# Up-projection of a channel mixer: products that go on accumulating in banks that were read, and sums moved from GpSimd to VectorE

## Chip, cores and metric

One core of one Trainium2 chip runs the kernel. The metric is the device time of one execution in microseconds (us); the profile is one execution with the hardware profiler on. Engines by their names in the profile: PE is TensorE, DVE is VectorE, ACT is ScalarE, POOL is GpSimd, SP the queue that issues most DMAs.

## What is computed

The reference is a trunk of two layers over 1024 tokens of 1024 channels, each layer a mixer and then a channel mixer, all in float32. The change is in the channel mixer, which runs once in each layer:

```
def conv_glu_ffn(x, w_up, conv_w, conv_b, w_down):
    h = causal_dwconv(x @ w_up, conv_w) + conv_b        # w_up 1024 x 5632, width-3 convolution over tokens
    gate, up = jnp.split(h, 2, axis=-1)                 # 2816 columns each
    return (jax.nn.silu(gate) * up) @ w_down            # w_down 2816 x 1024
```

## The kernel before

Each float32 product is made of three passes on TensorE: operands are split into a high part (a copy rounded to the engine's format, on ACT) and a low part (source minus high part, on DVE), and `mm3` multiplies high by high, high by low and low by high.

The up-projection (`ffn`) goes through 22 tiles, c = 0 to 21. A tile is 128 gate columns and 128 value columns. Taken as 2 x 2 blocks, it costs seven block products in place of eight (Winograd's form of Strassen's scheme), numbered 1 to 7. Each block product is four steps of `mm3`, so 12 matmuls of 128 x 128 by 128 x 512 into one PSUM bank of 512 columns; a tile has 84 of them. The operands of the tokens (B11, B21, B22, T1 to T4) are ready in SBUF. Of the weights, three products take a loaded block (A11, A12, A22) and four take a sum of blocks, S1 to S4, which `block` makes with `tensor_tensor` on GpSimd (line 249), 128 x 512 each. `prep` then splits the operand (ACT line 257, DVE line 258), five products ahead of its use (`FLA`).

In `product`, products 2 and 3 go to the two halves of a tile of two banks, `w["A"]`, that becomes the gate; the others go to single banks, of which the pool has four. The blocks of the result are sums of several products, and DVE makes these sums: seven adds of 128 x 512 with one operand in PSUM in each tile (lines 282 to 289, 294, 298), behind one copy on ACT (line 280). Then `conv` makes the convolution, once for the gate from PSUM and once for the value from SBUF: one activation on ACT (line 262) and two `scalar_tensor_tensor` of 128 x 1024 on DVE (lines 263 and 264). ACT applies SiLU to the gate (line 296), GpSimd multiplies gate and value (line 300, 128 x 1024) and issues the store (line 301).

Tiles 0 and 1 go side by side in the order `FIRST`, while the operands T1 to T4 of the last half of the tokens are still being made (line 148 and line 214, the latter on GpSimd for T3 and T4). From tile 2 on, tiles go one after the other, products in the order 1, 6, 5, 2, 7, 3, 4. Every engine runs its own instructions strictly in the order that the scheduler of the framework wrote at build time; waits between engines are semaphores, and two engines never work on the same PSUM bank at once. The down-projection (`dn`) follows with PE work of its own.

Of the kernel before, what the change touches and what calls it, by code (L numbers as in the profile page):

```python
# [16 lines left out]
P = 128  # L17
# [46 lines left out]
class Kern:  # L64
# [73 lines left out]
    def mm3(self, ps, ah, al, bh, bl, first, last):  # L138
        nc = self.nc
        nc.tensor.matmul(ps, ah, bh, start=first, stop=False)  # L140
        nc.tensor.matmul(ps, ah, bl, start=False, stop=False)  # L141
        nc.tensor.matmul(ps, al, bh, start=False, stop=last)  # L142

    def split_half(self, src, s="x"):
        """hi and lo of one [128, 512] operand, side by side."""
        t = self.U(s, F32R)
        self.nc.scalar.copy(t[:, :512], src)  # L147
        self.nc.vector.tensor_sub(t[:, 512:], src, t[:, :512].bitcast(F32))  # L148
        return t
# [34 lines left out]
    def mixer_operands(self, zs, half, gname, bname, xo):  # L184
        """the blocks B11, B21, B22 and sums T1 to T4 that the up-projection takes, in high and low parts"""
        nc = self.nc
        lo, hi = slice(0, 512), slice(512, 1024)
        raw = [self.U("xr") for _ in range(4)]
        ts = [self.U("xt") for _ in range(4)] if half else None

        def put(name, src):
            xo.setdefault(name, []).append(self.split_half(src, "x"))

        for j in range(4):
            for k in range(2):
                kt = j + 4 * k
                ps = self.B("tp")
                for i in range(4):
                    nc.tensor.transpose(ps[:, i * P:i * P + P], zs[i][:, kt * P:kt * P + P], self.ident)
                dst = raw[j][:, (lo, hi)[k]]  # L200
                nc.scalar.activation(dst, ps, AF.Identity, bias=self.pc_(bname, kt), scale=self.pc_(gname, kt))  # L201
                if not half:
                    put(("B11", "B21")[k], dst)
        if not half:
            xo["raw"] = raw
            return
        old = xo["raw"]
        for name, d, x, y in (("B22", None, None, None), ("T1", lo, (raw, lo), (old, lo)), ("T2", hi, (raw, hi), (ts, lo)),
                              ("T3", lo, (raw, hi), (raw, lo)), ("T4", hi, (ts, hi), (old, hi))):
            for j in range(4):  # L210
                if d is None:
                    put(name, raw[j][:, hi])
                    continue
                (nc.gpsimd if name in TP else nc.vector).tensor_tensor(ts[j][:, d], x[0][j][:, x[1]], y[0][j][:, y[1]], op=ALU.subtract)
                put(name, ts[j][:, d])

# [1 line left out]
    def ffn(self, l, xo, resid, tail, nxt=None):  # L218
        """generator, one step for each block product of the up-projection. That takes a gate tile and a value tile of
        128 columns together: as 2 x 2 blocks (columns by halves of the channels, times halves of the channels by  # L220
        halves of the tokens) they come from seven block products, by Winograd's form of Strassen's scheme."""
# [11 lines left out]
        def block(c, name):  # L233
            """a block of the weights, or a sum of such"""
# [7 lines left out]
            if name not in w:  # L242
                x, y, op = sums[name]
                x, y = block(c, x), block(c, y)
                half = ("S12", "S34")[name in ("S3", "S4")]
                if half not in w:
                    w[half] = self.U("ws")
                w[name] = w[half][:, lo if name in ("S1", "S3") else hi]
                nc.gpsimd.tensor_tensor(w[name], x, y, op=op)
# [17 lines left out]
        def product(c, i):  # L267
            w = W[c]
            xn = prods[i][1]
# [3 lines left out]
            t = w.pop(i)  # L273
            for j in range(4):
                k, x = j * P, xo[xn][j]
                self.mm3(ps, t[:, k:k + P], t[:, 512 + k:512 + k + P], x[:, lo], x[:, hi], j == 0, j == 3)
            add = nc.vector.tensor_add
# [7 lines left out]
            if i == 7:  # L285
# [4 lines left out]
                w["gate"] = True  # L290
            if i == 5:
                w["p5"] = ps
            if i in (3, 7) and "gate" in w and not any(k in w for k in (3, 7)):
                add(w["A"][:, hi], w["A"][:, hi], w["u"][:, hi])  # L294
                w["g"] = conv(w["A"], c)
                nc.scalar.activation(w["g"], w["g"], AF.Silu)
            if i == 4:
                nc.vector.tensor_sub(w["h"][:, lo], w["u"][:, lo], ps)
                v = conv(w["h"], NC + c)
                nc.gpsimd.tensor_tensor(v, w["g"], v, op=ALU.mult)  # L300
                nc.gpsimd.dma_start(GS[c], v)
                W[c].clear()

        seq = [(c, i) for i in FIRST for c in range(2)]
        seq += [(c, i) for c in range(2, NC) for i in (1, 6, 5, 2, 7, 3, 4)]
# [74 lines left out]
    def make_tail(self, gi, bi, row, mode):  # L380
        """gi, bi: parameter names; row: (g, b) DRAM rows. Returns (tail, result)."""
# [5 lines left out]
        def tail(t, r, dh):  # L387
            """goes on with half dh of a tile of tokens"""
# [50 lines left out]
    def out_proj(self, w, yhl, resid, tail, in_w=(0, 1, 7), eng=None):  # L439
        """generator: loads the weights, then goes on by tiles of 128 tokens"""  # L440
# [21 lines left out]
    def mixer0(self, then):  # L462
# [61 lines left out]
        # generators of filling work: each step is one half of a column tile of the input projection  # L524
# [51 lines left out]
        # attention, one tile of 128 queries of one head after the other  # L576
# [27 lines left out]
        def turn(hd, i, p):  # L604
            """the weights of one tile, keys first"""
# [54 lines left out]
        # operands of the output projection: the last head's come two tiles at a time  # L660
# [31 lines left out]
        # queries and keys of the first head follow the input as it arrives  # L692
# [68 lines left out]
    def rwkv(self, xf, then):  # L761
# [29 lines left out]
        def variant(i, kt, x=None, h=None, eng=None):  # L791
            """x plus its mixed difference to the token before: of all tokens, or of one half of them"""
# [8 lines left out]
        def ahead(items, make, n=2):  # L801
            """items with what make gives for them, n of these in the making before one is used"""
# [16 lines left out]
        def spread(xs, i, src=None):  # L819
            """generator: the operands of a projection"""  # L820
# [15 lines left out]
        def lora1(steps):  # L836
            """generator: the first products of several low-rank maps, over the channel tiles"""
# [18 lines left out]
        def loras():  # L856
            """generator: hidden parts of the gate, the decay and the learning rate; the small ones in several copies
            over the partitions, so that products of high and low parts go in one pass"""
# [21 lines left out]
        def project(xs, w, evac, by_half=False, ws=None, pair=True):  # L880
            """generator: one projection; stops between the halves of a tile and behind each tile, and says where. The
            first two tiles go side by side, so that they can follow the operands as these are made, and with pair
            the last two, so that they give the operands' room back one by one"""
# [58 lines left out]
        # receptance, with the loras between its tiles; its start fills the gap behind what comes before  # L942
# [33 lines left out]
        def gates():  # L976
            """generator: the gate, written out for later"""
# [28 lines left out]
        # second lora weights: high and low parts stacked against the doubled hidden rows  # L1006
# [156 lines left out]
        # Of the four pairs of heads in a unit, the first two (s = 0) keep the state, b and u in partitions 0 to 63  # L1163
        # and k and v in the others, the last two (s = 1) the other way round.
        def chunk_operands(q, g, s, a):
            """b and k of two pairs of heads, and a (or r) of each head with zeros beside it"""
# [14 lines left out]
        def prepare1(q, g, u):  # L1181
            """generator: chunk matrices of one unit between a and b, k, and the inverses of their 32x32 diagonal blocks"""
# [44 lines left out]
        def prepare3(q, g, u):  # L1227
            """generator: chunk matrices of one unit between r and b, k, and the transposes of b, k"""
# [18 lines left out]
        def prepare2(q, g, u):  # L1247
            """generator: the whole 64x64 inverses, and the operands of the recurrence"""
# [46 lines left out]
        def chunks(work, pump):  # L1295
            """one chunk of 64 tokens of each unit in work; the chains of two units run side by side"""
# [53 lines left out]
        def finish(q, g, O):  # L1350
            """generator: group norm over the 64 channels of each head, then bonus and gate"""
# [107 lines left out]
def build(tc, ins, out, stop=None):  # L1459
    with ExitStack() as ctx:  # L1460
# [18 lines left out]
        def mixed(i, l, w, resid, alpha, out_args, last_tail, nxt=None):  # L1479
            """the output projection of the mixer of layer l, with the start of its channel mixer in the gap behind"""  # L1480
# [131 lines left out]
```

## Time and profile before

| what | us |
|---|---|
| three runs | 2848.95, 2855.28, 2872.17 |
| median of the runs | 2855.28 |
| span of the profiled execution, first to last instruction | 2858.8 |
| up-projection, tiles 2 to 20, layer 0 | 607.7 to 994.7 of the span |
| up-projection, tiles 2 to 20, layer 1 | 2202.7 to 2590.3 of the span |

The span is the profiled execution's own time as far as the profile shows it; it lies 3.5 us above the median and within the runs. The two stretches of the up-projection are cut at the ACT copies of line 280, which stand right behind product 1 of a tile, so each holds 19 whole tile periods.

### The profile page before, as it was taken

How to read it: one execution, taken by the hardware profiler on the slowest of the kernel's cores; microseconds unless marked ns; L12 is line 12 of the kernel's file. 1: busy time of each engine (PE TensorE's matmuls, PEld its weight loads, DVE VectorE, ACT ScalarE, POOL GpSimd, SP SyncE). 2: the span in 40 equal slices, each digit the busy share in tenths (PEclk: the TensorE clock that was granted, in tenths of full speed). 3: DMA queues.
4: the chain of work that ended last, by engine and by line, in shares of the span. 5: the costliest groups of instructions: out<-in, count | busy, mean ns of one | idle time of the engine just before them, and what ended most of it. 6: DMA issues, size and time to landing. Idle time of an engine off the chain costs nothing. (4 is left out here: it accounts for less than half of the span.)

```text
span 2858.8 us, 38102 instructions
## 1 busy us (share of the span) xinstructions
PE 2639.9 (92%) x14736; PEld 2140.1 (75%) x14736; DVE 2065.9 (72%) x2796; ACT 1060.9 (37%) x1650; POOL 850.0 (30%) x558
## 2 busy tenths in 40 slices
PE   8999989979998999999998998688897999899998
PEld 6777777768777788777876777577776787778886
DVE  4645656699999964657778656777759999997463
ACT  3323343234343441526665223334224344334330
POOL 0000003564554303010045211345555455441000
PEclk9999979999999999999997998787998999999999
DMA  5111233122222173543256779777431222224751
GB/s 163 52 45 52 63 114 104 67 74 74 82 83 71 67 231 115 195 158 111 89 188 217 230 219 232 175 175 204 154 125 48 93 78 78 82 74 158 240 187 41
DMA packets 208678, 358.10 MB, mean 125 GB/s; under 512 B 88945, under 2 KB 118257, under 8 KB 208497
## 3 DMA queue, kind: packets, MB, share of 16 engines
q1 hardware_dynamic: 198704, 320.01, 36.1%
q0 software_dynamic: 9792, 35.66, 3.4%
q8 instruction: 116, 1.90, 0.3%
q14 instruction: 66, 0.53, 0.1%
HBM read 255.46 MB, written 95.94 MB: 123 GB/s over the span
## 5 line engine op out<-in xcount | busy, mean ns | idle before, releaser
L140 PE MATMUL up<-x,wu 128*128 128x512 f32 x1232 | 485.3, 397 | 47.4 <-DVE u L282 22.4
L142 PE MATMUL up<-x,wu 128*128 128x512 f32 x1232 | 479.0, 397 | 10.3 <-DVE wu L258 10.2
L141 PE MATMUL up<-x,wu 128*128 128x512 f32 x1232 | 486.1, 395 | 0.8 <-DVE x L148 0.7
L140 PEld LDWEIGHTS up<-x,wu 128*128 128x128 f32 x1232 | 234.5, 191 | 106.4 <-DVE up L284 26.7
L142 PEld LDWEIGHTS up<-x,wu 128*128 128x128 f32 x1232 | 234.7, 191 | 69.7 <-DVE wu L258 21.0
L300 POOL TENSOR_TENSOR cv<-cv,cv 128x1024 f32<-128x1024 f32 x44 | 161.3, 3665 | 413.5 <-DVE cv L264 362.6
L141 PE MATMUL dn<-wdl,gt 128*128 128x512 f32 x704 | 274.5, 390 | 0.7 <-DVE wdl L118 0.7
L140 PE MATMUL dn<-wdh,gt 128*128 128x512 f32 x704 | 273.9, 390 | 0.2 <-ACT xf L182 0.2
L141 PEld LDWEIGHTS up<-x,wu 128*128 128x128 f32 x1232 | 235.2, 191 | 51.2 <-DVE x L148 3.1
L142 PE MATMUL dn<-wdh,gt 128*128 128x512 f32 x704 | 271.2, 390 | 0.0
L258 DVE TENSOR_TENSOR wu<-wr,wu 128x512 fp32r<-128x512 f32 x132 | 223.8, 1716 | 6.4 <-ACT wu L257 6.4
L258 DVE TENSOR_TENSOR wu<-ws,wu 128x512 fp32r<-128x512 f32 x176 | 221.9, 1264 | 0.2 <-ACT wu L257 0.2
L118 DVE TENSOR_TENSOR wdl<-raw,wdh 128x1024 fp32r<-128x1024 f32 x88 | 116.5, 1324 | 100.6 <-ACT wdh L117 91.6
L262 ACT ACTIVATE cv<-up,par 128x1024 f32<-128x1024 f32 x44 | 53.1, 1207 | 363.1 <-DVE up L294 363.1
L141 PE MATMUL pr<-xv,wph 128*128 128x512 f32 x384 | 155.2, 404 | 6.1 <-DVE xv L816 4.2
L140 PE MATMUL pj<-x,wih 128*128 128x512 f32 x384 | 152.8, 408 | 7.7 <-ACT x L147 7.6
L140 PE MATMUL pr<-xv,wph 128*128 128x512 f32 x384 | 154.2, 406 | 5.8 <-DVE kp L1057 4.3
L142 PE MATMUL pr<-xv,wpl 128*128 128x512 f32 x384 | 155.2, 404 | 4.2 <-DVE wpl L118 4.2
L117 ACT CAST wdh<-raw 128x1024 fp32r<-128x1024 f32 x88 | 92.6, 1052 | 173.6 <-DMA raw<-wdn 108.7
L141 PEld LDWEIGHTS dn<-wdl,gt 128*128 128x128 f32 x704 | 132.5, 188 | 28.6 <-DVE wdl L118 1.1
L140 PEld LDWEIGHTS dn<-wdh,gt 128*128 128x128 f32 x704 | 132.6, 188 | 27.8 <-ACT xf L182 0.4
L142 PE MATMUL pj<-x,wil 128*128 128x512 f32 x384 | 153.2, 399 | 0.2 <-DVE wil L118 0.2
(301 smaller groups left out, 5700.6 us busy)
## 6 DMA issues: line engine op xcount, KB each, us to landing
wr<-wup SPq DMA_DIRECT2D x88, 512.0 KB, 3.6
raw<-wdn SPq DMA_DIRECT2D x88, 512.0 KB, 3.8
G<-cv POOLq DMA_DIRECT2D x44, 512.0 KB, 3.0
gr<-G SPq DMA_DIRECT2D x88, 256.0 KB, 3.8
bk<-bkS SPq DMA_DIRECT2D x32, 512.0 KB, 6.3
spill<-acc SPq DMA_DIRECT2D x24, 512.0 KB, 2.6
res<-spill SPq DMA_DIRECT2D x24, 512.0 KB, 4.8
raw<-win SPq DMA_DIRECT2D x22, 512.0 KB, 3.7
```

Of the source, the lines that this page charges most:

```text
L117: self.nc.scalar.copy(hi, raw)
L118: self.nc.vector.tensor_sub(lo, raw, hi.bitcast(F32))
L140: nc.tensor.matmul(ps, ah, bh, start=first, stop=False)
L141: nc.tensor.matmul(ps, ah, bl, start=False, stop=False)
L142: nc.tensor.matmul(ps, al, bh, start=False, stop=last)
L258: nc.vector.tensor_sub(t[:, hi], src, t[:, lo].bitcast(F32))
L262: nc.scalar.activation(cc, src, AF.Identity, bias=self.pc_(bname, ct), scale=self.pc_(wname, 88 + ct))
L300: nc.gpsimd.tensor_tensor(v, w["g"], v, op=ALU.mult)
```

## The change

In tiles 2 to 21 a product no longer has its own bank where the running sum can stay in PSUM. Product 2 accumulates onto product 1 in the first half of `A`; products 6, 5 and 3 accumulate in the second half of `A`; products 7 and 4 accumulate in one single bank `z`. Between these, DVE (or ACT) reads the bank while the sum is partial. So the order of the products is 1, 6, 2, 5, 7, 3, 4, and five adds on DVE stay of seven. For this the sign of T4 is turned. In tiles 0 and 1 (`apart`) the products go where they went. The sums S1 to S4 of the tiles from 2 on, and the product of gate and value of all tiles, are made by DVE in place of GpSimd.

```diff
@@ block
-                nc.gpsimd.tensor_tensor(w[name], x, y, op=op)
+                (nc.vector if c > 1 else nc.gpsimd).tensor_tensor(w[name], x, y, op=op)
@@ ffn
+        def multiply(c, i, ps, first=True, **kw):
+            t, x = W[c].pop(i), xo[prods[i][1]]
+            for j in range(4):
+                k = j * P
+                self.mm3(ps, t[:, k:k + P], t[:, 512 + k:512 + k + P], x[j][:, lo], x[j][:, hi], first and j == 0, j == 3, **kw)
...
+        def value(c):
+            w = W[c]
+            v = conv(w["h"], NC + c)
+            nc.vector.tensor_tensor(v, w["g"], v, op=ALU.mult)
+            nc.gpsimd.dma_start(GS[c], v)
+            w.clear()
...
+        def chained(c, i):
+            w = W[c]
+            if i == 1:
+                w["A"], w["u"] = self.A("up"), self.U("u2")
+            if i == 7:
+                w["z"] = self.B("up")
+            ps = w["z"] if i in (7, 4) else w["A"][:, lo if i in (1, 2) else hi]
+            multiply(c, i, ps, i in (1, 6, 7), skip_group_check=True)
+            if i == 1:
+                nc.scalar.copy(w["u"][:, lo], ps)
+            if i == 6:
+                add(w["u"][:, hi], w["u"][:, lo], ps)
+            if i == 5:
+                w["h"] = self.U("hv")
+                add(w["h"][:, hi], w["u"][:, lo], ps)
+            if i == 7:
+                add(w["h"][:, hi], w["h"][:, hi], ps)
+            if i == 3:
+                add(ps, ps, w["u"][:, lo])
+                gate(c)
+            if i == 4:
+                add(w["h"][:, lo], w["u"][:, hi], ps)
+                value(c)
...
-        seq += [(c, i) for c in range(2, NC) for i in (1, 6, 5, 2, 7, 3, 4)]
+        seq += [(c, i) for c in range(2, NC) for i in (1, 6, 2, 5, 7, 3, 4)]
```

## Rows read from the trace of the kernel before

**Rows 1.** The page: busy time by engine, and one of its groups of instructions.
```profile
PE 2639.9 (92%) x14736; PEld 2140.1 (75%) x14736; DVE 2065.9 (72%) x2796; ACT 1060.9 (37%) x1650; POOL 850.0 (30%) x558
...
L140 PE MATMUL up<-x,wu 128*128 128x512 f32 x1232 | 485.3, 397 | 47.4 <-DVE u L282 22.4
```
**Rows 2.** Busy time by stretch: stretch, length, busy us (instructions) by engine, clock, DMA.
```profile
core 0: us, PE busy (x) PEld busy (x) DVE busy (x) ACT busy (x) POOL busy (x), PEclk, DMA share, GB/s
607.70:652.00 44.30, 40.85 (x177) 32.74 (x176) 41.72 (x38) 17.08 (x25) 22.70 (x15) 1.00 0.26 96
652.00:994.70 342.70, 330.25 (x1417) 266.18 (x1417) 321.05 (x308) 131.16 (x189) 165.49 (x100) 0.99 0.23 77
2202.70:2248.40 45.70, 41.99 (x175) 33.58 (x174) 41.97 (x38) 17.01 (x24) 21.84 (x15) 0.96 0.26 92
2248.40:2590.30 341.90, 329.25 (x1418) 265.74 (x1417) 321.03 (x308) 131.26 (x189) 165.76 (x100) 0.99 0.24 77
...
2440.00:2480.00 40.00, 33.85 (x136) 26.77 (x135) 35.44 (x32) 15.43 (x22) 16.84 (x12) 0.91 0.24 79
```
**Rows 3.** Timeline of PE: start, us, first and 112th matmul of an unbroken run.
```profile
985.05 0.39 PE L140 MATMUL up<-x,wu 128*128 128x512 f32 x1
...
1010.28 0.39 PE L140 MATMUL dn<-wdh,gt 128*128 128x512 f32 x1
```
**Rows 4.** Timeline of DVE over one tile period; idle time before it in brackets.
```profile
2345.68 1.28 DVE L263 SCALAR_TENSOR_TENSOR cv<-up,par,cv 128x1023 f32<-128x1023 f32 x1 [1.28 <-ACT cv L262]
2346.89 1.28 DVE L263 SCALAR_TENSOR_TENSOR cv<-hv,par,cv 128x1023 f32<-128x1023 f32 x1
2348.08 1.28 DVE L264 SCALAR_TENSOR_TENSOR cv<-up,par,cv 128x1022 f32<-128x1022 f32 x1
...
2351.66 0.69 DVE L258 TENSOR_TENSOR wu<-ws,wu 128x512 fp32r<-128x512 f32 x1
2352.26 1.29 DVE L258 TENSOR_TENSOR wu<-wr,wu 128x512 fp32r<-128x512 f32 x2
...
2354.67 2.29 DVE L258 TENSOR_TENSOR wu<-ws,wu 128x512 fp32r<-128x512 f32 x1
2356.89 0.67 DVE L287 TENSOR_TENSOR u<-u,up 128x512 f32<-128x512 f32 x1
2357.48 4.17 DVE L258 TENSOR_TENSOR wu<-wr,wu 128x512 fp32r<-128x512 f32 x1
2361.58 0.67 DVE L288 TENSOR_TENSOR hv<-u,up 128x512 f32<-128x512 f32 x1
2362.18 0.67 DVE L289 TENSOR_TENSOR u<-u,up 128x512 f32<-128x512 f32 x1
...
2363.37 0.68 DVE L294 TENSOR_TENSOR up<-up,u 128x512 f32<-128x512 f32 x1
2365.33 1.28 DVE L263 SCALAR_TENSOR_TENSOR cv<-up,par,cv 128x1023 f32<-128x1023 f32 x1 [1.27 <-ACT cv L262]
...
2368.92 0.68 DVE L282 TENSOR_TENSOR u<-u,up 128x512 f32<-128x512 f32 x1
```
**Rows 5.** Timeline of POOL in the same period.
```profile
2351.89 4.52 POOL L300 TENSOR_TENSOR cv<-cv,cv 128x1024 f32<-128x1024 f32 x1 [8.72 <-DVE cv L264]
...
2357.33 1.30 POOL L249 TENSOR_TENSOR ws<-wr,wr 128x512 f32<-128x512 f32 x1
2358.57 1.28 POOL L249 TENSOR_TENSOR ws<-wr,ws 128x512 f32<-128x512 f32 x1
```
**Rows 6.** Groups of instructions on DVE in the down-projection, 2620 to 2800.
```profile
L118 DVE TENSOR_TENSOR wdl<-raw,wdh 128x1024 fp32r<-128x1024 f32 x39 | 47.7, 1223 | 55.5 <-ACT wdh L117 47.7 <-issue 3.9 <-PE dn L141 2.2
```
**Rows 7.** Timeline of PE at a long wait of the up-projection.
```profile
2459.81 0.80 PE L140 MATMUL up<-x,wu 128*128 128x512 f32 x1 [4.59 <-DVE up L284]
```
**Rows 8.** Timeline of DVE in tiles 0 and 1 of layer 0.
```profile
584.12 5.09 DVE L148 TENSOR_TENSOR x<-xt,x 128x512 fp32r<-128x512 f32 x3
589.13 1.27 DVE L282 TENSOR_TENSOR u<-u,up 128x512 f32<-128x512 f32 x2
```
**Rows 9.** Timeline of POOL in the same stretch.
```profile
585.29 1.71 POOL L249 TENSOR_TENSOR ws<-wr 128x512 f32<-128x512 f32 x1
587.07 1.59 POOL L249 TENSOR_TENSOR ws<-ws,wr 128x512 f32<-128x512 f32 x1
```

More of the change, by code (lines that the diff above doesn't have):

```diff
@@ L136, in load_split2, with mm3 @@
         return hi, lo
-    def mm3(self, ps, ah, al, bh, bl, first, last):
+    def mm3(self, ps, ah, al, bh, bl, first, last, **kw):
         nc = self.nc
-        nc.tensor.matmul(ps, ah, bh, start=first, stop=False)
-        nc.tensor.matmul(ps, ah, bl, start=False, stop=False)
-        nc.tensor.matmul(ps, al, bh, start=False, stop=last)
+        nc.tensor.matmul(ps, ah, bh, start=first, stop=False, **kw)
+        nc.tensor.matmul(ps, ah, bl, start=False, stop=False, **kw)
+        nc.tensor.matmul(ps, al, bh, start=False, stop=last, **kw)
     def split_half(self, src, s="x"):
@@ L208, in mixer_operands @@
         for name, d, x, y in (("B22", None, None, None), ("T1", lo, (raw, lo), (old, lo)), ("T2", hi, (raw, hi), (ts, lo)),
-                              ("T3", lo, (raw, hi), (raw, lo)), ("T4", hi, (ts, hi), (old, hi))):
+                              ("T3", lo, (raw, hi), (raw, lo)), ("T4", hi, (old, hi), (ts, hi))):
             for j in range(4):
@@ L265, in conv, with gate, apart @@
             return cc
-        def product(c, i):
-            w = W[c]
-            xn = prods[i][1]
+        def multiply(c, i, ps, first=True, **kw):
[3 more added lines that the diff above has]
+                self.mm3(ps, t[:, k:k + P], t[:, 512 + k:512 + k + P], x[j][:, lo], x[j][:, hi], first and j == 0, j == 3, **kw)
+        add = nc.vector.tensor_add
+        def gate(c):
+            w = W[c]
+            w["g"] = conv(w["A"], c)
+            nc.scalar.activation(w["g"], w["g"], AF.Silu)
+        def value(c):
[4 more added lines that the diff above has]
+            w.clear()
+        def apart(c, i):
+            w = W[c]
             if i == 2:
@@ L272, in product @@
             ps = w["A"][:, lo] if i == 2 else w["A"][:, hi] if i == 3 else self.B("up")
[L273 to L277, printed above, removed]
+            multiply(c, i, ps)
             if i == 1:
@@ L289, in product @@
                 add(w["u"][:, hi], w["u"][:, hi], w["p5"])
-                w["gate"] = True
+                add(w["A"][:, hi], w["A"][:, hi], w["u"][:, hi])
+                gate(c)
             if i == 5:
                 w["p5"] = ps
[L293 to L296, printed above, removed]
             if i == 4:
[L298 to L302, printed above, removed]
+                add(w["h"][:, lo], w["u"][:, lo], ps)
+                value(c)
+        def chained(c, i):
+            w = W[c]
+            if i == 1:
[15 more added lines that the diff above has]
+                add(ps, ps, w["u"][:, lo])
+                gate(c)
+            if i == 4:
+                add(w["h"][:, lo], w["u"][:, hi], ps)
+                value(c)
+        def product(c, i):
+            (apart if c < 2 else chained)(c, i)
         seq = [(c, i) for i in FIRST for c in range(2)]
-        seq += [(c, i) for c in range(2, NC) for i in (1, 6, 5, 2, 7, 3, 4)]
+        seq += [(c, i) for c in range(2, NC) for i in (1, 6, 2, 5, 7, 3, 4)]
         for c in range(2):
```

## The prediction

> **What bounds the kernel now.** I read the page first. PE is busy 92% of the span and DVE 72%, which says little of any one stage; but the largest group of PE idle time, 47.4 us ahead of up-projection matmuls, ends at DVE instructions [rows 1]. So the next view was busy time by stretch, over the two up-projections alone. From tile 4 on, DVE is busy 321 of 342 us in each layer, that is 94%, and PE completes some 1417 matmuls in 342.7 us, 0.242 us each [rows 2]. What PE can do is seen at the end of the same stage, where 111 matmuls run from 985.05 to 1010.28 without a break: 0.2273 us each [rows 3]. A tile of 84 matmuls would then take 19.09 us. Seventeen tile periods would take 324.6 us where they take 342.7 and 341.9: 18.1 and 17.3 us are lost there. Tiles 2 and 3 take 44.3 and 45.7 us against 38.2: 6.1 and 7.5 us are lost [rows 2].
>
> The timeline of DVE over one tile shows why. From one gate convolution to the next are 19.65 us, 0.56 more than PE needs, with a single idle gap of 1.27 us, a wait for ACT [rows 4]. So DVE sets the period here. Most DVE instructions follow each other at a fixed step: 0.60 us for a split or an add of 128x512, 1.19 us for a convolution pass [rows 4]. Two splits on line 258 do not: from 2354.67 and 2357.48 the next start is 2.22 and 4.10 us later, 1.62 and 3.50 us too much, 5.12 us in all [rows 4]. In these times GpSimd multiplies gate and value (2351.89 for 4.52 us) and makes weight sums (2357.33 and 2358.57, 1.30 and 1.28 us) [rows 5]. The adds with an operand in PSUM keep 0.60 us; it is the splits, with both operands in SBUF, that stretch. Account of the tile: 7 splits and 7 adds at 0.60 are 8.40, 4 passes at 1.19 are 4.76, 1.28 wait, 5.12 stretch: 19.56, against 19.65 measured.
>
> Where DVE falls further behind, PE waits longer and then runs at the lower of its two levels (1.2 GHz in place of 2.4): behind a wait of 4.59 us the matmul at 2459.81 took 0.80 us where 0.39 is usual, and the granted clock of that stretch is 0.91 [rows 2, 3, 7].
>
> **The change, part by part.** *Fewer adds.* Two of seven go from each chained tile: 2 x 0.60 = 1.20 us less on DVE. *Sums on DVE.* Four of 128x512 with both operands in SBUF; the nearest row is the split, 0.60 us: 2.40 us more. *Gate product on DVE.* 128x1024, both operands in SBUF: the nearest row is the low-part split of the down-projection, 1.223 us [rows 6], say 1.20 at its step: 1.20 us more. GpSimd loses all its arithmetic of these tiles, so the stretch of 5.12 us has nothing left to cause it. DVE by tile: 8.40 + 4.76 - 1.20 + 2.40 + 1.20 = 15.56, with the wait of 1.28 at most 16.84 us. That is 2.25 us under PE's 19.09. PE becomes the bound; its own work does not change (84 matmuls by tile before and after), and a different accumulate flag on a matmul adds none. The store stays on GpSimd's queue and is now released by DVE, earlier, with nothing queued behind it; its reader comes in the next stage. The sign of T4 and the sums of tiles 0 and 1 cost the same as before.
>
> The Trainium skill, Perfetto Trace Analysis, section Optimizing Scalar/DVE Operations, gives advice in the other direction: when DVE is saturated, offloading from it may make sense, and the change loads it; by that advice alone a tile would come to the 22.0 us of the third rival below, not to 19.1. The same section says that the two engines share a read port, and by SBUF — State Buffer, section SBUF: two separate sides, a GpSimd instruction and a DVE one with two SBUF operands exclude each other for a whole instruction; the stretched splits and the unstretched adds agree with that.
>
> *New waits.* Three products now write a bank that somebody must have read: product 2 behind ACT's copy of 1, product 5 behind DVE's add of 6, product 3 behind the add of 5; and product 4 behind the add of 7. In each case one other product, 12 x 0.2273 = 2.73 us, lies between. The tight one is product 5, since the add of 6 comes right behind the convolutions of the tile before. By hand, from the end of product 3 as zero: its add ends at 0.9, ACT's pass at 2.1, then four DVE passes (4.76), the add of product 4 (0.60) and the gate product (1.20) fit until 8.7, with splits in the holes; product 6 of the next tile ends at 8.2, its add at 9.4 or, if three more sums and splits stand ahead of it (1.8), at 11.2. Product 5 wants to start at 10.9. So the wait costs 0 to 0.4 us by tile. In the order of before, the add of 6 stands 5.55 us behind the gate's add (2363.37 to 2368.92), ahead of the last pass [rows 4], which speaks for the near end; I take 0.1. In 40 tiles: 4 us, bounds 0 and 16. Queued behind product 5 is all of PE.
>
> *Tiles 0 to 3.* PE's waits for line 282, 22.4 us in the kernel [rows 1], lie mostly in tiles 0 and 1. In front of it three splits of the token operands take 5.01 us in place of 1.8, and GpSimd makes sums of tile 2 from 585.29 on, the ones that move [rows 8, 9]. Without these, 3.2 us at most come back in a layer, at worst none; I take 2.5 and the same for layer 1: 5 us. In tiles 2 and 3 DVE has a backlog of two convolutions and two gate products from tiles 0 and 1. The moved work costs it 3.6 us less 1.2 by tile, and the stretch of about 5.1 by tile goes: 2.7 less by tile, but the gate products of tiles 0 and 1 (2.4) come on top. About 3 us of the 6.1 and 7.5 lost come back; I take 3.4 by layer, 6.8, bounds 0 and 13.6.
>
> *Sum.* 18.1 + 17.3 + 5 + 6.8 - 4 = 43.2 us off the span of 2858.8 leaves 2815.6; the median of the runs lies 3.5 lower, so 2812. Ends: all returned and no waits, 35.4 + 6.4 + 13.6 = 55.4, 2800; nothing in tiles 0 to 3 and 0.4 us waits, 35.4 - 16 = 19.4, 2836. Nothing later takes it back: the next stage starts on PE without a gap [rows 3] and loads its weights in its own time.
>
> **The rivals.** *Readers late.* The order written for DVE or ACT puts the reading instruction one or two further back (a pass or a sum with a split, about 1 us by tile in place of 0.1). 40 us go of the 47.2: 2848, no change that can be told; about 1% is what this kernel's runs can resolve. For it: every engine is in order, and the margin by hand is 1.5 us at best; a bank waits for just one reader now, where four single banks gave several products of slack. Against: DVE has 2.25 us to spare by tile.
>
> The Trainium skill, PSUM — Partial Sum Buffer, section Summary: rules for kernel authors, tells to read PSUM from another bank than the one that matmuls are running into; here the next product is bound for the bank just read. By it this rival and the next are the outcome; the trace of before has no such product to show it.
>
> *Slower: the chain of waits is the bound.* Should the add of 6 be queued behind the next tile's first two sums and their split too (1.8 us), and product 3 or 4 meet a similar delay, PE stands 2.2 us by tile: 88 us against 47.2 gained, 2896. It decides from 47.2 / 40 = 1.2 us by tile. Against: these sums belong to a later step of the program than the add.
>
> *DVE stays the bound.* If the stretched splits have another cause than the moved work, each tile gets 2.4 us longer on DVE, 22.0, and 40 tiles give 2855 + 96 = 2951. Against: the stretch stands only where GpSimd computes, and only on splits.
>
> **How the numbers follow.** Forecast 0.66, readers late 0.21, chain 0.10, DVE 0.03. The range 2799 to 2845 holds the forecast's ends and about half of the first rival. The forecast's own range crosses the 1% line, 2827, with some 0.05 of its chance: faster 0.62, same 0.25, slower 0.13.
>
> **What would show it.** Right: in the stretches of tiles 4 to 20 the tile period is 19.1 to 19.2, matmuls at 0.227; DVE's splits all take 0.68, DVE is busy about 80%, and GpSimd nearly idle; PE's waits end at ACT or PE work no more than briefly. Wrong: a repeated PE gap ahead of product 5 (or 2, 3, 4) that ends at a DVE add or ACT copy, a clock below 1.00 behind such gaps, or splits that stay at 2 to 4 us.

## The result, and the profile after

The changed kernel took 2895.95 us (2891.02 to 2904.54) against 2852.11 for the kernel before on the same chip: 1.0149 times, 95% interval 1.0121 to 1.0176. It is slower, where 2812 us was forecast. The profiled execution spans 2902.6 us, 43.8 more than before. Of all executions of the runs below, one (7249.77 us, of the early sums) was disturbed as a whole and is left out of the comparisons.

The page of the kernel after: busy time by engine, and the first groups of instructions, to be read beside [rows 1].

```profile
PE 2648.9 (91%) x14736; PEld 2127.4 (73%) x14736; DVE 1954.7 (67%) x2920; ACT 1069.3 (37%) x1650; POOL 461.2 (16%) x354
...
L140 PE MATMUL up<-x,wu 128*128 128x512 f32 x1232 | 492.3, 402 | 59.5 <-DVE hv L329 28.1
L142 PE MATMUL up<-x,wu 128*128 128x512 f32 x1232 | 487.1, 396 | 25.9 <-DVE wu L258 25.9
```

GpSimd's busy time went from 850.0 to 461.2 us, and VectorE's fell too, from 2065.9 to 1954.7, though VectorE was given work. So the stretch of its splits is gone (0.68 to 0.69 us each in the rows below). But TensorE's idle time ahead of these matmuls rose from 47.4 to 59.5 us on line 140 and from 10.3 to 25.9 on line 142. The add of line 329 is new as a releaser: it is the reader behind product 5, where a reader is an instruction of VectorE or ScalarE that reads a bank while its sum is partial. The split of line 258 was a releaser before too, with 10.2 us. The row of line 142 in the page before:

```profile
L142 PE MATMUL up<-x,wu 128*128 128x512 f32 x1232 | 479.0, 397 | 10.3 <-DVE wu L258 10.2
```

Busy time by stretch after, tiles 4 to 20 of each layer, cut as in [rows 2]:

```profile
650.80:1012.80 362.00, 337.14 (x1430) 262.19 (x1429) 271.33 (x358) 134.42 (x189) 9.03 (x17) 1.00 0.20 74
2272.40:2634.30 361.90, 337.00 (x1430) 262.19 (x1429) 271.34 (x358) 134.38 (x189) 9.04 (x17) 1.00 0.20 74
```

Seventeen periods take 362.0 and 361.9 us in place of 342.7 and 341.9: 21.29 us a tile, 2.2 over what 84 matmuls need. VectorE is now busy for 75% of the stretch, TensorE for 93% and GpSimd for 2%, and the clock stays at 1.00. The two stretches together are 39.3 us longer than before, nearly the whole loss. Neither VectorE nor TensorE is saturated here: the stage is bound by a chain of waits.

Timeline of TensorE over one such tile, 693 to 716, the two matmuls with an idle gap ahead of them, each with the matmul before it:

```profile
704.85 0.39 PE L142 MATMUL up<-x,wu 128*128 128x512 f32 x1
706.02 0.50 PE L140 MATMUL up<-x,wu 128*128 128x512 f32 x1 [0.78 <-DVE hv L329]
...
711.90 0.40 PE L141 MATMUL up<-x,wu 128*128 128x512 f32 x1
712.98 0.50 PE L142 MATMUL up<-x,wu 128*128 128x512 f32 x1 [0.68 <-DVE wu L258]
```

Timeline of VectorE in the same tile:

```profile
703.21 0.69 DVE L258 TENSOR_TENSOR wu<-ws,wu 128x512 fp32r<-128x512 f32 x1 [1.48 <-ACT wu L257]
705.27 0.69 DVE L329 TENSOR_TENSOR hv<-u,up 128x512 f32<-128x512 f32 x1 [1.37 <-PE up L142]
706.00 0.69 DVE L331 TENSOR_TENSOR hv<-hv,up 128x512 f32<-128x512 f32 x1
709.07 0.70 DVE L333 TENSOR_TENSOR up<-up,u 128x512 f32<-128x512 f32 x1 [2.39 <-PE up L142]
709.68 0.68 DVE L249 TENSOR_TENSOR ws<-wr,wr 128x512 f32<-128x512 f32 x1
710.27 0.69 DVE L249 TENSOR_TENSOR ws<-wr,ws 128x512 f32<-128x512 f32 x1
711.04 1.28 DVE L263 SCALAR_TENSOR_TENSOR cv<-up,par,cv 128x1023 f32<-128x1023 f32 x1
712.24 0.68 DVE L258 TENSOR_TENSOR wu<-ws,wu 128x512 fp32r<-128x512 f32 x1
```

Three steps are to be followed. At 705.27 VectorE had been idle, waiting for product 5; it read the bank, and TensorE, idle too, went on at 706.02 with product 3 into the same bank. Two engines took turns, with no other work to cover the wait. The second add, line 331, followed at 706.00 without a wait: its product 7 was long done (TensorE had run it ahead of 6, as shown below). And at 712.98 a matmul of the third pass waited for the low part of its operand, whose split ran at 712.24, behind the gate's add of 709.07.

The order in which the built program issues the products on TensorE explains the first. In the steady state, with c the tile:

```
written in the source:   1(c) 6(c) 2(c) 5(c) 7(c) 3(c) 4(c)
issued on TensorE:       7(c) 6(c) 1(c+1) 2(c) 5(c) 3(c) 4(c) 7(c+1) ...
```

The order is counted off the trace. Each product is 12 matmuls; line 324 reads product 1, and lines 326, 329, 331, 333 and 336 read products 6, 5, 7, 3 and 4. Product 5 ends where line 329 starts (705.27), and the 12 matmuls from 706.02 on end where line 333 starts (709.07), so they are product 3. The scheduler moved product 7 ahead of 6 and drew product 1 of the next tile forward. What was to stand between 5 and 3 is no longer there.

### The profile page after: what moved, and what is told of

Its sections match the earlier page's. It is cut to its first block, busy times and chain, and to the rows that moved or that the text cites. A ratio compares the mean times of both kernels' runs of the same rounds, so it can differ in the third digit from the quotient of the medians.

```text
span 2902.6 us, 37665 instructions
## 1 busy us (share of the span) xinstructions
PE 2648.9 (91%) x14736; PEld 2127.4 (73%) x14736; DVE 1954.7 (67%) x2920; ACT 1069.3 (37%) x1650; POOL 461.2 (16%) x354
## 5 line engine op out<-in xcount | busy, mean ns | idle before, releaser
L140 PE MATMUL up<-x,wu 128*128 128x512 f32 x1232 | 492.3, 402 | 59.5 <-DVE hv L329 28.1
L142 PE MATMUL up<-x,wu 128*128 128x512 f32 x1232 | 487.1, 396 | 25.9 <-DVE wu L258 25.9
L257 ACT CAST wu<-ws 128x512 fp32r<-128x512 f32 x176 | 104.6, 618 | 239.2 <-DVE ws L249 137.3
L258 DVE TENSOR_TENSOR wu<-ws,wu 128x512 fp32r<-128x512 f32 x176 | 136.0, 775 | 54.0 <-ACT wu L257 54.0
L284 POOL DMA_DIRECT2D G<-cv x44 | 23.7, 539 | 895.9 <-DVE cv L283 895.9
L140 PE MATMUL pj<-x,wih 128*128 128x512 f32 x384 | 153.0, 409 | 7.6 <-ACT x L147 7.6
L141 PE MATMUL pj<-x,wih 128*128 128x512 f32 x384 | 154.1, 401 | 0.0
```

The source lines that it names most:

```text
L140: nc.tensor.matmul(ps, ah, bh, start=first, stop=False, **kw)
L141: nc.tensor.matmul(ps, ah, bl, start=False, stop=False, **kw)
L142: nc.tensor.matmul(ps, al, bh, start=False, stop=last, **kw)
L257: nc.scalar.copy(t[:, lo], src)
L258: nc.vector.tensor_sub(t[:, hi], src, t[:, lo].bitcast(F32))
```

## The experiments

There are nine runs, each beside runs of the kernel before on its own chip. Tile periods are taken as above, over tiles 4 to 20 of layer 0. The question is which part of the change costs: the moved work (theory B) or the accumulation behind readers (theory A), and if the latter, which of its waits. In the diffs, a line of dots stands for lines left out.

**Engines alone.** Into the kernel before, only the two moves:

```diff
-                nc.gpsimd.tensor_tensor(w[name], x, y, op=op)
+                (nc.vector if c > 1 else nc.gpsimd).tensor_tensor(w[name], x, y, op=op)
-                nc.gpsimd.tensor_tensor(v, w["g"], v, op=ALU.mult)
+                nc.vector.tensor_tensor(v, w["g"], v, op=ALU.mult)
```

> The kernel before with only the engine moves: sums of tiles from 2 on and the gate product on VectorE, products in banks of their own as before. Theory A (the accumulating products make TensorE wait for readers): without them VectorE has 18.0 us of work in a tile against 19.1 of TensorE, so a tile takes 19.1 to 19.5 and the kernel 2805 to 2825. Theory B (sums and gate product in VectorE's queue are what costs): a tile takes 20.5 or more, the kernel 2875 or more.

Measured: 2803.53 us, 0.9818 times the kernel before (0.9798 to 0.9838). Busy time by stretch, tiles 2 and 3 and tiles 4 to 20 of layer 0:

```profile
601.90:641.80 39.90, 39.90 (x178) 33.04 (x177) 37.67 (x50) 17.53 (x26) 1.84 (x3) 1.00 0.31 107
641.80:965.50 323.70, 323.70 (x1430) 268.04 (x1429) 287.14 (x392) 129.49 (x189) 9.03 (x17) 1.00 0.24 82
```

TensorE is busy in every microsecond: 19.04 us a tile, where [rows 3] gave 19.09 as the bound. VectorE has 287.14 / 17 = 16.9 us of work in a tile, 89%. The time lies just below the range of theory A, which had put VectorE's work at 18.0. Theory B falls: the moves alone are the gain that the prediction saw. This version beats both kernels.

**Accumulation alone.** The changed kernel with both moves undone (the two lines above the other way round).

> The changed kernel with sums and gate product back on GpSimd: only the accumulation in read banks is left of the change. Theory A: the wait of product 3 for the add behind product 5 stays, about 1 us in a tile, so a tile takes 20.0 to 20.5 and the kernel 2860 to 2880. Theory B: the waits come from the moved work, so a tile takes 19.6 or less and the kernel 2850 or less.

Measured: 2930.42 us, 1.0271 times (1.0234 to 1.0308); 21.79 us a tile, above the range that theory A gave. Tiles 4 to 20 of layer 0:

```profile
657.90:1028.30 370.40, 335.41 (x1429) 264.08 (x1428) 285.53 (x273) 136.28 (x188) 135.51 (x100) 1.00 0.20 71
```

The accumulation alone loses more than the whole change. In each tile TensorE waits 0.8 us for the reader behind 5, as in the changed kernel, and 1.3 us for a split, as in the next run.

**Sums back.** The changed kernel with the sums of all tiles on GpSimd, the gate product on VectorE.

> The changed kernel with the weight sums alone back on GpSimd, the gate product on VectorE. Theory A with two waits in a tile (about 1 us for the add behind product 5, about 1 us for the split of S3, which stands behind a waiting add in VectorE's queue): the second goes, so a tile takes 20.2 and the kernel 2858 to 2870. If the sums have no part in it: 21.3 in a tile, 2896 as the changed kernel.

Measured: 2924.48 us, 1.0251 times (1.023 to 1.0273); 21.79 us a tile. Both expectations missed: the second wait did not go, it grew. Timelines of GpSimd, ScalarE, VectorE and TensorE in one tile of this run, in this order:

```profile
705.17 1.30 POOL L249 TENSOR_TENSOR ws<-wr,wr 128x512 f32<-128x512 f32 x1
```
```profile
715.14 1.21 ACT L262 ACTIVATE cv<-up,par 128x1024 f32<-128x1024 f32 x1 [6.63 <-DVE up L333]
716.24 1.13 ACT L257 CAST wu<-ws 128x512 fp32r<-128x512 f32 x2
```
```profile
717.58 0.68 DVE L336 TENSOR_TENSOR hv<-u,up 128x512 f32<-128x512 f32 x1
718.17 0.68 DVE L258 TENSOR_TENSOR wu<-ws,wu 128x512 fp32r<-128x512 f32 x1
```
```profile
718.91 0.50 PE L142 MATMUL up<-x,wu 128*128 128x512 f32 x1 [1.28 <-DVE wu L258]
```

The sum S3 is there by 706.5, but ScalarE rounds it at 716.24 only: in ScalarE's order the cast stands behind the gate's convolution pass, which had waited 6.63 us for the gate's add. So it was not the place of the sum in VectorE's queue, as I had it, but the cast's place behind a waiting pass on ScalarE; with product 7 drawn forward on TensorE, only product 4 is left to cover the way from gate add over pass, cast and split.

**Single banks.** The changed kernel with each running sum in a single bank of its own, so that the two halves of the gate are no longer one tile while products run into them. The gate is put together in SBUF, by one more copy on ScalarE.

```diff
-            if i == 1:
-                w["A"], w["u"] = self.A("up"), self.U("u2")
-            if i == 7:
-                w["z"] = self.B("up")
-            ps = w["z"] if i in (7, 4) else w["A"][:, lo if i in (1, 2) else hi]
+            bank = {1: "y", 2: "y", 6: "q", 5: "q", 3: "q", 7: "z", 4: "z"}[i]
+            if i in (1, 6, 7):
+                w[bank] = self.B("up")
+            if i == 1:
+                w["u"] = self.U("u2")
+            ps = w[bank]
...
+            if i == 2:
+                w["A"] = self.U("ga")
+                nc.scalar.copy(w["A"][:, lo], ps)
...
-                add(ps, ps, w["u"][:, lo])
+                add(w["A"][:, hi], w["u"][:, lo], ps)
```

> The changed kernel with each running sum in a single bank of its own (products 1 and 2, products 6, 5 and 3, products 7 and 4), so that no product waits for a reader of the other half of a two-bank tile; the gate goes to SBUF by one more copy on ScalarE. If the waits come from the two halves of the gate's tile being one thing to the waits: a tile takes 19.1 to 19.8 and the kernel 2805 to 2840. If accumulating behind a reader costs as such: 21 or more in a tile, 2885 or more.

Measured: 2838.0 us, 0.9941 times (0.9921 to 0.9962); 20.22 us a tile. The kernel's time is at the far end of the first expectation, the tile between the two. Tiles 4 to 20 of layer 0:

```profile
640.70:984.50 343.80, 332.98 (x1436) 266.80 (x1435) 268.80 (x358) 142.79 (x206) 9.06 (x17) 1.00 0.21 77
```

The wait for a reader is gone; of the gaps on TensorE one is left in each tile:

```profile
720.14 0.50 PE L142 MATMUL up<-x,wu 128*128 128x512 f32 x1 [0.68 <-DVE wu L258]
```

This run does not tell banks from order, because the scheduler's order changed with the banks. Timeline of VectorE, with a split of a weight sum, the reader of product 5 (line 332) and that of product 3 (line 336):

```profile
709.55 0.69 DVE L258 TENSOR_TENSOR wu<-ws,wu 128x512 fp32r<-128x512 f32 x1 [0.74 <-ACT wu L257]
...
710.76 0.68 DVE L332 TENSOR_TENSOR hv<-u,up 128x512 f32<-128x512 f32 x1
...
716.14 0.69 DVE L336 TENSOR_TENSOR ga<-u,up 128x512 f32<-128x512 f32 x1 [3.50 <-PE up L142]
```

The readers are 5.38 us apart, two products of 12 matmuls, where they were 3.80 apart in the changed kernel (705.27 and 709.07). So one product now runs between 5 and 3 and covers the reader. By its operand, split at 709.55 just ahead of it, it is product 6 of the next tile. The next two runs hold the order fixed.

**Order of the program.** The changed kernel with TensorE's order bound to that of the source; an edge of order without a semaphore joins the first step of each product to the last of the one before.

```diff
+                with self.tc.issue_after(last[0]) if last and c > 1 and not j else ExitStack():
+                    ins = self.mm3(ps, ...)
+            last[:] = [ins.ins]
```

Here `mm3` also returns its last matmul, and the arguments of the call are left out.

> The changed kernel with TensorE bound to the order of the program, 1, 6, 2, 5, 7, 3, 4, which the prediction took for granted, by order alone and no new wait. If waits go bank by bank, as the prediction had it, each reader has a product of cover: 19.1 to 19.5 in a tile, the kernel 2810 to 2825. If waits take the two-bank tile of the gate as one thing, product 6 waits for the copy behind 1 and product 2 for the add behind 6, each right behind it, about 1 us each: 20.9 to 21.3 in a tile, the kernel 2880 to 2900.

Measured: 2915.58 us, 1.0196 times (1.0162 to 1.023); 21.72 us a tile, above both expectations. Tiles 4 to 20 of layer 0, and TensorE in one tile:

```profile
648.70:1018.00 369.30, 334.04 (x1428) 265.42 (x1428) 274.04 (x358) 136.44 (x189) 9.06 (x17) 1.00 0.20 72
```

```profile
736.22 0.50 PE L140 MATMUL up<-x,wu 128*128 128x512 f32 x1 [0.86 <-ACT u L328]
740.46 0.50 PE L140 MATMUL up<-x,wu 128*128 128x512 f32 x1 [1.22 <-DVE u L330]
```

This is the order that the prediction reckoned with, and it is no faster. Product 6, into the second half of the tile, waits for the copy that reads product 1 in the first half, and product 2, into the first half, for the add that reads product 6 in the second. The waits count the two-bank tile as one thing. The miss above the range is in part a queue: the add starts about half a microsecond after product 6 ends (739.24), behind a pass and a sum on VectorE:

```profile
739.12 0.68 DVE L249 TENSOR_TENSOR ws<-wr 128x512 f32<-128x512 f32 x1
739.73 0.68 DVE L330 TENSOR_TENSOR u<-u,up 128x512 f32<-128x512 f32 x1
```

These waits for the other half are what the scheduler's other order had avoided, at the price of 5 next to 3.

**Single banks and order of the program**, both edits together.

> The kernel with running sums in single banks and in addition TensorE bound to the order of the program, so that each reader has a product of cover and product 7 comes two products later, behind the split of S3. If the order of the products is what left 20.2 us in a tile there: 19.05 to 19.3 in a tile, the kernel 2800 to 2815. If accumulating behind a reader still costs: 20 or more, 2835 or more.

Measured: 2809.89 us, 0.9832 times (0.979 to 0.9875). Tiles 4 to 20 of layer 0:

```profile
640.40:964.10 323.70, 323.70 (x1430) 268.04 (x1429) 273.15 (x358) 146.30 (x206) 9.06 (x17) 1.00 0.22 82
```

Again 19.04 us a tile, with TensorE never idle. Against the run before, the order is the same and the place of the running sums differs (with the gate in SBUF and its one more copy on ScalarE): 21.72 against 19.04 us. Accumulating in a bank that was read in between costs nothing as such here, if the reader has one product of cover. Nor does it gain anything beyond the engines alone (0.9818 times, 19.04 us a tile): TensorE is the bound in both, so two adds less on VectorE are worth nothing here.

**Gate product alone.** The kernel before with only the gate product on VectorE (the second pair of lines of the first diff).

> The kernel before with the gate product alone on VectorE; sums stay on GpSimd, banks as before. GpSimd keeps some 5.5 of its 9 us in a tile. If VectorE's stretch goes in proportion, it falls from 5.1 to about 3 us: VectorE then has 13.2 + 1.3 + 1.2 + 3 = 18.7 us in a tile, under TensorE's 19.05, and the kernel takes 2805 to 2825. If the sums stretch VectorE as much as both did: 20.9 in a tile, 2890.

Measured: 2816.73 us, 0.9851 times (0.9829 to 0.9874), in the expected range; 19.42 us a tile, 0.38 above TensorE's bound. One moved instruction a tile brings most of the gain; the sums that stay still stretch splits, one of them to 4.72 us beside three sums on GpSimd:

```profile
712.92 4.72 DVE L258 TENSOR_TENSOR wu<-ws,wu 128x512 fp32r<-128x512 f32 x1
```
```profile
713.29 1.30 POOL L249 TENSOR_TENSOR ws<-wr,wr 128x512 f32<-128x512 f32 x1
714.54 1.30 POOL L249 TENSOR_TENSOR ws<-wr,ws 128x512 f32<-128x512 f32 x1
715.79 1.29 POOL L249 TENSOR_TENSOR ws<-wr 128x512 f32<-128x512 f32 x1
```

**Early sums.** The changed kernel with S3 and S4 made with S1 and S2, tried while the place of the sums was still thought to be the cause of the second wait.

```diff
                 src = block(c, prods[i][0])
+                if c > 1 and i == 6:
+                    for name in ("S1", "S3", "S4"):
+                        block(c, name)
```

> The changed kernel with S3 and S4 made right behind S1 and S2, a product earlier in VectorE's order, so that they no longer stand behind the add of product 3. TensorE's order shifts a little with it: product 7 now starts with two matmuls between products 5 and 3. Theory (two waits in a tile, one for the add behind product 5, one for the split of S3): the second goes and the first is covered by the two matmuls in part, so a tile takes 19.5 to 20.2 and the kernel 2825 to 2865. If the split of S3 is late for another reason, 21 in a tile and 2885 or more.

Measured: 2998.15 us, 1.049 times (1.0452 to 1.0527), a bad miss. The same kernel once more, for its trace:

> The kernel with early S3 and S4 once more, for a profile: the one before was of a disturbed execution. Its times were near 2998, some 3.6 us in a tile over the kernel before. In its order of instructions VectorE has the add behind product 7 ahead of the gate's add, and product 7 is cut in two around product 3. Theory: product 3 waits for the add behind 5, the rest of 7 for a split that stands behind that add, and product 4 right behind 7 for the add of 7: three waits with nothing to cover them, some 23 us in a tile, the kernel 2980 to 3010.

Measured: 3003.77 us, 1.0528 times (1.0446 to 1.0609); 23.88 us a tile. The time is in the range, but not for the waits that I named. TensorE, over one tile:

```profile
700.20 0.50 PE L140 MATMUL up<-x,wu 128*128 128x512 f32 x1 [0.71 <-ACT wu L260]
708.35 0.50 PE L140 MATMUL up<-x,wu 128*128 128x512 f32 x1 [2.13 <-DVE u L329]
714.79 0.50 PE L140 MATMUL up<-x,wu 128*128 128x512 f32 x1 [0.71 <-ACT wu L260]
```

The largest is for the add behind product 6, which here stands behind the gate product and the sums on VectorE, and two are for casts. Two instructions earlier in the source gave a new order of instructions and cost 2.6 us a tile more than the change itself. Why the scheduler chose it stays open.

## Why the prediction was wrong

*What bounds the kernel now*: right. VectorE set the period of 19.65 us, and GpSimd's work stretched its splits. With that work gone the splits take 0.68 us in the changed kernel, and the engines-only run sits at TensorE's bound.

*The prices of the moved work*: right. The sum at 0.60 and the gate product at 1.20 us by tile, with the two adds kept, make 16.76 us of VectorE's work in a tile; the engines-only run shows 16.9. The Trainium skill's advice (Perfetto Trace Analysis, Optimizing Scalar/DVE Operations) to take work off a saturated DVE, and with it the third rival, did not hold here: the moved work replaced a larger stretch. Its reservation, that the two engines share a read port, fits the runs better.

*New waits*: this step failed, in two places. "In each case one other product ... lies between" took the order of the source for the order of the engine. The built program issues product 3 right behind 5, so the add between them is bare: TensorE idles 0.78 us, and from one matmul start to the next 1.17 us pass in place of 0.227. The wait that I called tight, product 5 for the add of 6, was not the one that cost. And I took the waits to go bank by bank. In this program they go by tile: bound to the order of the source, the kernel loses 2.7 us a tile in waits for readers of the other half, and with the halves in tiles of their own it loses nothing. A row that I quoted showed this: in [rows 7] product 3, into the second half, is released by the add of line 284 in the first half. I read there the length of the wait, and not who waited for whom.

The term was put at 0.1 us by tile, 4 us in all, with 0.4 as the far end. It measured 2.25 us, 21.29 against 19.04: about 0.94 for the reader behind 5 (1.17 less 0.227), 0.85 for the late split of product 7 (1.08 from 711.90 to 712.98, less 0.227), the rest in small gaps and in the slower matmuls right behind the waits (0.50 us in place of 0.39). In 40 tiles that is 90 us, against 47.2 reckoned as gain.

*The second rival*, the chain of waits, put exactly that price: 2.2 us by tile and 2896 us, at a chance of 0.10. That it came out so closely is luck. It was right that waits of some 2 us by tile, over its threshold of 1.2, would bind the stage, but it saw readers queued late on VectorE. In the changed kernel VectorE was idle for 1.37 us ahead of the reader behind 5, which came at once and had no cover; and the other wait was for the split of an operand, which the rival does not have. I held it unlikely because of the order of instructions in the source.

The section Summary: rules for kernel authors of PSUM — Partial Sum Buffer (the Trainium skill) advises a different bank for reading while matmuls run. The runs agree with it. In the run with single banks in program order each reader works while matmuls run into another bank, at 19.04 us a tile; in the changed kernel TensorE has no other bank to turn to between 5 and 3, and stands idle for 0.78 us. The prediction said in that place that the next product is bound for the bank just read. In the order that it reckoned with, this was not so.

*Tiles 0 to 3*: of the 11.8 us taken, the changed kernel got next to nothing back in tiles 2 and 3 (44.1 us in place of 44.3 in layer 0), as their chain of waits began there; the engines-only run got 4.4 us there (39.9). Tiles 0 and 1 gave nothing back either: from their first copies of product 1 to that of tile 2, layer 0 takes 56.7 us before, 56.8 in the changed kernel and 53.7 both in the engines-only run and in the one with single banks in program order. Why the changed kernel has no gain there stays open.

## What to carry to other kernels

Before an accumulator is shared between engines, list in the order that is really issued who writes, who reads, who writes next, and what covers each reader; the order of the source is no evidence when a scheduler stands between. Give each running sum a tile of its own, if waits are kept by tile. And when VectorE is at its limit beside a working GpSimd, look first whether single instructions are stretched: moving GpSimd's work onto the full engine took 1.8% off this kernel, one moved product 1.5%.

## What was not expected of the hardware

Moving work onto an engine that was busy 94% of a stretch made that engine less busy: 321 us in 17 tiles before, 287 in the engines-only run, with 3.6 us more of instructions in each tile. And a bare hand-over from TensorE to VectorE and back, for one add of 0.69 us, cost TensorE 0.94 us; in the run bound to program order the two waits for the other half cost 0.86 and 1.22 us of idle time.
